# Moving five gate chunks of the first branch beside the attention in quarters three and four of a three-branch trunk layer

## The chip, the cores and the metric

The kernel runs on one core of a Trainium2 chip. The metric is device time in microseconds of one execution. The kernel before took 2836.89 us (median of three runs, 2834.71 to 2837.46). A difference of about 0.2% (5.7 us) is what a measurement of this kernel can tell from no change.

## The reference, cut to what matters

One layer runs over 2048 tokens of width 1024 with 16 meta tokens put in front. The normed tokens are projected once; three causal mixers of four heads (head size 128) work on the pieces, and each mixer's result goes through its own output matrix, is multiplied by a sigmoid gate, and is summed:

```
xn   = rms_norm(h);  proj = xn @ w_in
o_sb = stick_breaking_attention(q, k, v) * silu(sb_z)       # mixer 0: all earlier keys
o_gd = rms_norm(gated_delta_rule(q, k, v, beta, g)) * silu(gd_z)   # mixer 1: state over chunks
o_hg = rms_norm(hgrn2(q, k, v, log f)) * silu(hg_z)         # mixer 2: state over chunks
gate = sigmoid(mix)                                         # three of width 1024
y    = gate0 * (o_sb @ P0) + gate1 * (o_gd @ P1) + gate2 * (o_hg @ P2)
out  = h + y @ w_out
```

In the attention the work of a query block grows with the number of keys before it, so the later a quarter of the sequence, the longer its attention. The queries and keys of the delta rule go through a short causal convolution, which is VectorE work.

## The kernel before, in words

The tokens go through in four quarters of 512 (`nq` is 4, `TQ` is 512). Within a quarter two streams of work are woven together.

The first stream is dense work, the generator `dense_work`. It is cut into chunks: `proj` (a chunk is 24 matmuls of 512 columns; three matmuls per block of 128 make up for the precision of one, `mm3`, lines 166 to 169). In order: the attention's four projections for each head (`sb_proj`), a small projection for the delta rule's rates (`gdn_rows`, evacuated at L628), the delta rule's query, key and value chunks with their convolutions (`gdn_proj` with `conv`: twelve chunks, evacuated by ScalarE at L725, then three VectorE multiply-adds each at L730 and a product at L734), the first branch (`branch` with b = 0), the delta rule's gates (`gdn_gates`), the projections of the third mixer (`hg_proj`, evacuated at L1046, L1058 and L1064) with pieces of branch one between them, branch two, and the output matrix (`outp`).

A `branch` has, for each of eight output blocks, a gate chunk (24 matmuls; the sigmoid on ScalarE at L1203 puts it into a tile) and a product (12 matmuls of the mixer's result with the output matrix, at L1217 multiplied by the gate). With `lag` of 0 gate and product of a block follow each other; with a `lag` of 4, as branch two has, four gates run ahead of the first product. In the first branch the gates lie in tiles of the tag "g", of which there are two, and the product writes y, which has the tag "y" with eight tiles. The products of the first branch need the attention of all four heads (`obs`).

The second stream is the scans: the attention (`sb_scan`: scores `z` on TensorE, sigmoids on ScalarE at L522 and L523, a scan on VectorE at L528, a product at L534 on VectorE or GpSimd, transposes `tr` at L558, the split into high and low part on ScalarE at L562 and VectorE at L118, and the products `av`), then the delta rule (`gdn_mats`; `gdn_scan` with the inversion of small matrices on VectorE, written to and read from memory at L899 and L902, transposed at L904, then block products at L920, L941, L944, L959 and L969, and the recurrence over four steps of 128 tokens at L991, L996, L1002 to L1005), and the third mixer (`hg_scan`).

Every dense piece ends by yielding `END`. The main loop at the end of the kernel says how many dense pieces are emitted beside each scan: `adv(n)` emits n pieces alone, `weave(scan, scan_us, n)` spreads n pieces over a scan in proportion to the table `US` of their costs. The order in which the code emits is a priority only: a scheduler then lists each engine's instructions by it and by its own model of when operands and tiles are free, and on the chip each engine runs its list in order. So a piece for which no tile is free stands later in the list than where it was emitted.

The tiles that matter: "D" (16 tiles of a quarter's row of 512 tokens, used by nearly every projection, among them the raw results of L628 and L725 and the evacuations of L1046, L1058 and L1064), "S" (21, used by the scans), "w2" (5 tiles of weights, 512 KB each, loaded by SyncE's queue at L140), three matmul result tiles "acc" and one "av" in PSUM.

## Time and profile before

| | |
|---|---|
| median of three runs | 2836.89 us |
| the profiled execution, its own time | 2834.65 us |
| its span, first to last instruction | 2832.9 us |
| TensorE busy (PE) | 2777.6 us, 98% |
| VectorE busy (DVE) | 1501.6 us, 53% |
| ScalarE busy (ACT) | 934.1 us, 33% |
| GpSimd busy (POOL) | 737.7 us, 26% |
| mean granted TensorE clock | 0.996 |
| quarters, by the last output addition at L1255 | end at about 702, 1372, 2082 and 2830 us |
| attention, by the sigmoids at L522 | 1402 to 1652 us in quarter three, 2112 to 2405 us in quarter four |
| convolutions, by L730 | 1531 to 1644 us in quarter three, 2262 to 2384 us in quarter four |

Times in the profile are from the span's start. PE is TensorE, PEld its weight loads, DVE VectorE, ACT ScalarE, POOL GpSimd, SP SyncE's queue of transfers. In a row of windows stand the stretch, its length and each engine's busy time in it with the count of instructions, then the granted clock, the share of the DMA engines and GB/s. A row of waits names who waited for whom, the total, the number of times and the longest. A row of the timeline has start, duration, the instruction, how many were merged, and in brackets the idle time before it with what ended it. Matmuls overlap: a record runs past the start of the next one.

### The profile page before, as it was taken

What the parts mean: (1) busy time and instruction counts of PE and PEld (TensorE: products, weight loads), DVE (VectorE), ACT (ScalarE), POOL (GpSimd) and SP (SyncE); (2) the same over time, 40 slices, a digit from 0 to 9 for tenths busy, and PEclk for the clock granted to TensorE, in tenths of its full rate; (3) what the DMA queues carried; (4) which work ended last, traced back from release to release, by engine and by line L of the source; (5) the groups of instructions that cost most, each with busy time, mean ns of one, the idle gap of its engine ahead of it and who ended that gap; (6) DMA issues with size and microseconds to landing.
All of it is one profiled execution on the core that took longest, in us unless ns stands there. A gap on an engine that the chain in (4) does not pass through costs nothing. (4 is left out here: it accounts for less than half of the span.)

```text
span 2832.9 us, 42113 instructions
## 1 busy us (share of the span) xinstructions
PE 2777.6 (98%) x15696; PEld 2318.5 (82%) x15696; DVE 1501.6 (53%) x2879; ACT 934.1 (33%) x2131; POOL 737.7 (26%) x1009
## 2 busy tenths in 40 slices
PE   7999999999999999999999999999999999999999
PEld 7898788888887888888887778888888777788887
DVE  5466638745367535543256754464325677627521
ACT  5554333243345212112244531211224555112110
POOL 4555214433132302112023330111212323302111
PEclk9999999999999999999999999999999999999999
DMA  7667746679554654447654356344764434653456
GB/s 261 230 210 242 257 153 212 228 249 323 186 172 151 193 163 134 149 141 248 228 179 159 132 167 183 119 146 144 245 209 149 135 116 139 206 151 124 152 155 209
DMA packets 199632, 520.64 MB, mean 184 GB/s; under 512 B 42432, under 2 KB 43520, under 8 KB 199428
## 3 DMA queue, kind: packets, MB, share of 16 engines
q1 hardware_dynamic: 199140, 517.88, 56.1%
q8 instruction: 124, 2.03, 0.3%
q14 instruction: 80, 0.66, 0.1%
q10 hardware_dynamic: 288, 0.07, 0.0%
HBM read 397.55 MB, written 120.31 MB: 183 GB/s over the span
## 5 line engine op out<-in xcount | busy, mean ns | idle before, releaser
L167 PE MATMUL acc<-xh,w 128*128 128x512 f32 (+2 forms) x2224 | 853.5, 384 | 5.9 <-DMA w<-wk 1.7
L168 PE MATMUL acc<-xl,w 128*128 128x512 f32 (+2 forms) x2224 | 837.8, 377 | 0.3 <-DVE xl L260 0.2
L169 PE MATMUL acc<-xh,w 128*128 128x512 f32 (+2 forms) x2224 | 836.2, 376 | 0.7 <-DVE w L118 0.7
L167 PEld LDWEIGHTS acc<-xh,w 128*128 128x128 f32 x2224 | 421.9, 190 | 80.5 <-DMA w<-wk 2.5
L169 PEld LDWEIGHTS acc<-xh,w 128*128 128x128 f32 x2224 | 421.5, 190 | 74.3 <-DVE w L118 1.4
L168 PEld LDWEIGHTS acc<-xl,w 128*128 128x128 f32 x2224 | 421.8, 190 | 68.4 <-DVE xl L260 1.3
L528 DVE TENSOR_TENSOR_SCAN S<-S,zero 128x128 f32<-128x128 f32 (+4 forms) x216 | 196.8, 915 | 129.3 <-ACT S L522 116.8
L118 POOL TENSOR_TENSOR w<-wraw,w 128x512 fp32r<-128x512 f32 x106 | 150.1, 1417 | 292.8 <-ACT w L147 262.1
L534 POOL TENSOR_TENSOR S<-S,S 128x256 f32<-128x256 f32 (+2 forms) x108 | 93.3, 864 | 355.9 <-DVE S L528 262.2
L147 ACT CAST w<-wraw 128x512 fp32r<-128x512 f32 x182 | 112.4, 618 | 140.0 <-PE acc L169 67.6
L522 ACT ACTIVATE S<-z,rq 128x128 f32<-128x128 f32 (+4 forms) x216 | 116.8, 541 | 125.8 <-PE z L169 80.4
L730 DVE SCALAR_TENSOR_TENSOR D<-D,cw,D 128x512 f32<-128x512 f32 (+1 forms) x144 | 123.8, 860 | 18.0 <-ACT D L728 15.9
L167 PE MATMUL av<-xh,w 128*128 128x512 f32 (+2 forms) x328 | 128.8, 393 | 1.1 <-ACT D L1050 1.1
L167 PE MATMUL acc<-ob,w 128*128 128x512 f32 x316 | 126.8, 403 | 2.1 <-ACT ob L401 1.4
L168 PE MATMUL av<-xl,w 128*128 128x512 f32 (+2 forms) x328 | 127.7, 389 | 0.0
L118 DVE TENSOR_TENSOR S<-tr,S 128x512 fp32r<-128x512 f32 (+4 forms) x176 | 104.9, 606 | 41.6 <-ACT S L562 41.2
L169 PE MATMUL av<-xh,w 128*128 128x512 f32 (+2 forms) x328 | 126.9, 387 | 0.0
L168 PE MATMUL acc<-ob,w 128*128 128x512 f32 x316 | 125.4, 398 | 0.0
L169 PE MATMUL acc<-ob,w 128*128 128x512 f32 x316 | 124.9, 396 | 0.0
L1221 POOL TENSOR_TENSOR y<-y,g 128x512 f32<-128x512 f32 x32 | 45.8, 1436 | 272.7 <-DVE g L1219 272.7
L523 ACT ACTIVATE S<-z,rq 128x128 f32<-128x128 f32 (+4 forms) x216 | 116.2, 538 | 1.0 <-POOL S L527 0.9
L562 ACT CAST S<-tr 128x512 fp32r<-128x512 f32 (+4 forms) x176 | 91.0, 529 | 63.0 <-PE tr L558 62.8
(384 smaller groups left out, 5039.4 us busy)
## 6 DMA issues: line engine op xcount, KB each, us to landing
w<-wk SPq DMA_DIRECT2D x555, 512.0 KB, 3.5
wk<-w SPq DMA_DIRECT2D x184, 512.0 KB, 3.5
wraw<-in_w_in_dram SPq DMA_DIRECT2D x142, 256.0 KB, 3.8
D<-in_xq_dram SPq DMA_DIRECT2D x56, 256.0 KB, 4.5
S<-rows SPq DMA_DIRECT2D x48, 256.0 KB, 4.9
S<-dv SPq DMA_DIRECT2D x48, 256.0 KB, 4.2
out_dram<-D SPq DMA_DIRECT2D x32, 256.0 KB, 4.7
S<-dk SPq DMA_DIRECT2D x24, 264.0 KB, 3.9
```

The lines of the kernel that those rows point to most:

```text
L118: (eng or nc.gpsimd).tensor_sub(out_, a, hi.bitcast(F32))
L147: nc.scalar.copy(hi, raw)
L167: nc.tensor.matmul(dst, lh, rh, start=first, stop=False)
L168: nc.tensor.matmul(dst, lh, rl, start=False, stop=False)
L169: nc.tensor.matmul(dst, ll, rh, start=False, stop=last)
L522: nc.scalar.activation(pc[:, :n], z[:, :n], AF.Sigmoid, scale=rq[:, NT + i : NT + i + 1])
L523: nc.scalar.activation(at[:, :n], z[:, :n], AF.Sigmoid, scale=rq[:, i : i + 1])
L528: nc.vector.tensor_tensor_scan(pc[:, 0:n][:, ::-1], pc[:, 0:n][:, ::-1], zero1.broadcast_to([P, n]), 1.0 if carry[i] is None else pc[:, n ...
L534: eng.tensor_mul(at[:, :n], at[:, :n], pc[:, 1 : n + 1])
L562: nc.scalar.copy(ath[:kw, cs_], tr[:kw, cs_])
L730: nc.vector.scalar_tensor_tensor(dst[:, c0:], raw[:, c0 + i : c0 + i + n], cw[:, ci, i : i + 1], dst[:, c0:], ALU.mult, ALU.add)
L1221: nc.gpsimd.tensor_add(y[e], y[e], g)
```

## The change

In quarters three and four (`AHEAD` is 2, so for j of 2 and 3) the first branch gets a lag of 5. Its first five gate chunks are emitted right behind the attention's projections, ahead of `gdn_rows` and `gdn_proj`; then, behind the delta rule's projections, three more pieces (gates five to seven with products zero to two), and behind the first `hg_proj` the five products that are left. The gates of these two quarters lie in "y" tiles, and the product is written over the gate. In quarters one and two everything stays. The main loop gets other counts in those quarters and the table of costs a second version, one after the other for two quarters each.

```
+        tag = "D" if b == 2 else ("y" if lag else "g")
+
         def gate(e):
-            gs[e] = slot("D", (P, TQ)) if b == 2 else slot("g", (P, TQ))
+            gs[e] = slot(tag, (P, TQ))
...
             if b == 0:
-                y[e] = slot("y", (P, TQ))
+                y[e] = g if lag else slot("y", (P, TQ))
                 nc.vector.tensor_mul(y[e], g, ps)
...
+    AHEAD = 2
...
+            ahead = 5 * (j >= AHEAD)
+            b0 = branch(j, xs, 0, obs, y, yh, yl, ahead)
+            yield from take(b0, ahead)
             yield from gdn_rows(j, xs, gst)
             yield from gdn_proj(j, xs, range(H), gst)
             pool_share[0] = 2
-            b0 = branch(j, xs, 0, obs, y, yh, yl)
-            yield from take(b0, 5)
+            yield from take(b0, 3 if ahead else 5)
             yield from gdn_gates(j, xs, range(H), gst)
-            yield from take(b0, 3)
+            if not ahead:
+                yield from take(b0, 3)
             yield from hg_proj(j, xs, 0, hst)
+            if ahead:
+                yield from take(b0, 5)
             b1 = branch(j, xs, 1, obs, y, yh, yl)
...
+    ) * AHEAD + (
+        [CHUNK_US] * 34 + [B_US] * 3 + [CHUNK_US] * 8 + [3 * END] * 5 + [CHUNK_US] * 4 + [B_US] * 2 + REST
+    ) * (nq - AHEAD)
...
-        us = sum((US + US)[ends[0] % len(US) :][:n])
+        us = sum(US[ends[0] :][:n])
...
+        adv(5 * (j >= AHEAD))
         for h in range(H):
             weave(gdn_mats(j, h, gst), 8.0, 3)
...
-        adv(5)
+        adv(4 if j >= AHEAD else 5)
...
-        adv(5)
+        adv(6 if j >= AHEAD else 5)
```

What this does to the lists of TensorE in quarter four is seen at two places. The first is in the attention of the second head. `acc` is the result of a dense chunk, `z`, `tr` and `av` are the attention's scores, transposes and value products; `xh` and `xl` are the normed tokens, `w` the weights. Before:

```order
L169 MATMUL z_21252<-S_21174,D_20356 128x512
L168 MATMUL acc_22232<-xl_20106,w_4570_22230 128x512
L169 MATMUL acc_22232<-xh_20105,w_4570_22230 128x512
L168 MATMUL av_20969<-S_21205,S_21043 128x512
L169 MATMUL av_20969<-S_21204,S_21044 128x512
L558 MATMUL tr_21272<-ident,S_21054 128x128
L558 MATMUL tr_21272<-ident,S_21080 128x128
```

Now, at the same scores (`z` is of the same step):

```order
L169 MATMUL acc_22230<-xh_19983,w_4560_22228 128x512
L167 MATMUL z_21244<-S_21166,D_20347 128x512
L168 MATMUL z_21244<-S_21167,D_20347 128x512
L167 MATMUL av_20961<-S_21196,S_21035 128x512
L169 MATMUL z_21244<-S_21166,D_20348 128x512
L167 MATMUL acc_22230<-xh_20021,w_4560_22228 128x512
L168 MATMUL acc_22230<-xl_20022,w_4560_22228 128x512
L169 MATMUL acc_22230<-xh_20021,w_4560_22228 128x512
L167 MATMUL acc_22230<-xh_20059,w_4560_22228 128x512
L168 MATMUL av_20961<-S_21197,S_21035 128x512
```

Before, `acc_22232` is the first convolution's chunk, and behind its last matmul 99 rows of attention follow without a dense one, up to the second convolution's chunk. Now `acc_22230` is a gate chunk, the second of five, and the longest run of attention rows without a dense one in this quarter has 35. The last value product of the fourth head stands at row 11020 before, with three gate chunks of the first branch ahead of it, and at row 11156 now, with eight.

The second place is in the delta rule's scan of quarter four, at its block products. Before, with `acc_24555` and `av_24632` two chunks of the third mixer's first head:

```order
L169 MATMUL acc_24555<-xh_20105,w_5019_24553 128x512
L167 MATMUL av_24632<-xh_19839,w_5035_24628 128x512
L969 MATMUL z_24158<-S_22977,S_23965 64x64 x4
L969 MATMUL tr_24169<-S_23393,S_23966 64x64 x4
L991 MATMUL z_24200<-Sg_404,S_22947 128x128
L991 MATMUL tr_24202<-Sg_405,S_23145 128x128
L168 MATMUL av_24632<-xl_19840,w_5035_24628 128x512
L169 MATMUL av_24632<-xh_19839,w_5035_24628 128x512
```

Now, with `acc_24768` the last chunk for which a result tile is left:

```order
L168 MATMUL acc_24768<-xl_20098,w_5043_24766 128x512
L169 MATMUL acc_24768<-xh_20097,w_5043_24766 128x512
L959 MATMUL z_24190<-S_24042,S_23124 64x64 x4
L959 MATMUL z_24190<-S_24042,S_23322 64x64 x4
L959 MATMUL tr_24200<-S_24043,S_23540 64x64 x4
L959 MATMUL tr_24200<-S_24043,S_23739 64x64 x4
L969 MATMUL z_24216<-S_23124,S_24042 64x64 x4
L969 MATMUL tr_24227<-S_23540,S_24043 64x64 x4
L991 MATMUL z_24251<-Sg_404,S_23094 128x128
L991 MATMUL tr_24253<-Sg_405,S_23292 128x128
```

Behind these, the scan's 76 rows from L959 up to the last step's L996 stand without a dense matmul between them; before, the longest such run in this scan has 31 rows, the third step and the first half of the fourth. In quarter three the longest such run has 42 rows now and 31 before.

## The prediction

> **What bounds the kernel now.** I read the page first, then the windows by stage, then what TensorE waited for in the stages where it stood idle, then the timeline there. The page:

> ```profile
> span 2832.9 us, 42113 instructions
> PE 2777.6 (98%) x15696; PEld 2318.5 (82%) x15696; DVE 1501.6 (53%) x2879; ACT 934.1 (33%) x2131; POOL 737.7 (26%) x1009
> ```

> TensorE is busy for all but 55 us, so the change, which adds and removes no matmul, can win only where TensorE waits. The windows of quarters three and four (stretch, length, then busy time of PE, PEld, DVE, ACT, POOL, the granted clock, DMA share and GB/s) say where that is:

> ```profile
> core 0: us, PE busy (x) PEld busy (x) DVE busy (x) ACT busy (x) POOL busy (x), PEclk, DMA share, GB/s
> ...
> 1402.00:1519.00 117.00, 117.00 (x621) 96.64 (x621) 64.20 (x97) 54.48 (x115) 28.40 (x55) 1.00 0.52 176
> 1519.00:1663.00 144.00, 136.79 (x690) 109.34 (x688) 101.03 (x161) 77.75 (x166) 43.59 (x83) 0.99 0.40 133
> 1663.00:2112.00 449.00, 447.53 (x2505) 371.99 (x2506) 202.92 (x445) 84.11 (x216) 79.72 (x100) 1.00 0.57 178
> 2112.00:2216.00 104.00, 103.95 (x538) 84.92 (x537) 60.90 (x87) 50.36 (x100) 29.40 (x49) 1.00 0.50 163
> 2216.00:2249.00 33.00, 30.28 (x162) 23.68 (x161) 20.71 (x33) 17.80 (x38) 8.33 (x18) 1.00 0.28 97
> 2249.00:2317.00 68.00, 64.69 (x326) 52.27 (x325) 49.99 (x75) 39.48 (x80) 19.50 (x36) 1.00 0.45 148
> 2317.00:2334.00 17.00, 14.26 (x75) 10.84 (x75) 14.48 (x22) 10.00 (x22) 3.55 (x13) 0.90 0.09 32
> 2334.00:2384.00 50.00, 47.66 (x235) 38.36 (x234) 40.32 (x56) 29.80 (x60) 17.19 (x23) 1.00 0.46 155
> 2384.00:2414.00 30.00, 28.50 (x153) 22.66 (x151) 15.27 (x27) 13.40 (x31) 4.38 (x13) 1.00 0.39 118
> 2414.00:2833.00 419.00, 413.84 (x2342) 343.87 (x2342) 184.78 (x416) 68.47 (x189) 74.49 (x90) 1.00 0.53 166
> ```

> The first 117 us of quarter three's attention and the first 104 of quarter four's have no idle TensorE: attention projections stand beside them. Idle time comes later, 7.2 us in quarter three (144.00 - 136.79) and 2.7, 3.3, 2.7, 2.3 and 1.5 = 12.5 us in quarter four. Behind the attentions it is 1.5 us in 449 and 5.2 in 419. So the change is played for some 20 us.

> Two of these windows have a cause that the change touches. In 2216 to 2249 the DMA engines carry 97 GB/s and in 2317 to 2334 only 32: no weights are read, since no dense chunk stands in the list there. The timeline shows why in the first of them:

> ```profile
> 2218.92 0.39 PE L623 MATMUL acc<-xl,w 128*128 128x512 f32 x1
> 2245.97 0.29 PE L169 MATMUL z<-S,D 128*128 128x272 f32 x1
> 2247.05 0.59 ACT L628 COPY D<-acc 100x512 f32<-100x512 f32 x1
> ```

> The rates' chunk ends its matmuls at about 2219, and its evacuation into a "D" tile runs 28 us later, right behind the second head's last scores, which read that head's queries out of a "D" tile. All 16 are held, so the dense stream stands still, and TensorE has only the attention, each step of which it then waits for:

> ```profile
> PE av L168 <- DVE S L118: 1.5, 4, 0.7
> PE z L167 <- ACT S L523: 0.7, 1, 0.7
> PE av L167 <- ACT S L562: 0.4, 2, 0.2
> ```

> **The change part by part.** *The gates in the hole.* Gate chunks evacuate into "y" tiles, which nobody holds then, and need no "D". A gate costs TensorE 24 matmuls, and the timeline gives their spacing:

> ```profile
> 2333.72 0.39 PE L167 MATMUL acc<-xh,w 128*128 128x512 f32 x1
> 2333.95 0.39 PE L168 MATMUL acc<-xl,w 128*128 128x512 f32 x1
> ```

> 0.23 us apart, so a chunk is 5.5 us and five are 28 us, which take nothing off and add nothing: they are only done elsewhere. In the list the 99 rows without a dense matmul are gone. What that saves is the waiting in that window: 2.7 us of idle time, plus what the idle time hides. A record is 0.39 us though the next could start after 0.23, so each of the seven waits loses 0.16 us more: 1.1 us. Sum 3.8 us; bounds 2 and 4.

> *The second hole*, 2317 to 2334, has 55 such rows before and at most 35 now. It has 2.7 us idle and four waits (0.6 us), and a slow clock:

> ```profile
> PE tr L558 <- POOL S L534: 1.7, 1, 1.7
> 2331.80 0.63 PE L168 MATMUL acc<-xl,w 128*128 128x512 f32 x1
> 2332.23 0.63 PE L169 MATMUL acc<-xh,w 128*128 128x512 f32 x1
> ```

> Matmuls start 0.43 us apart, for about five of them: 1.0 us more. Sum 4.3 us; as a run of 35 rows stays, I take three quarters, 3.2 us, with bounds 0 and 5. [...]

> *The convolutions.* They are put later, not away. Their VectorE price stays:

> ```profile
> L730 DVE SCALAR_TENSOR_TENSOR D<-D,cw,D 128x512 f32<-128x512 f32 x36 | 29.9, 832 | 2.5 <-ACT D L728 1.9
> PE av L168 <- DVE S L118: 2.9, 2, 1.6
> ```

> The second row is of 1519 to 1663: the low part of the weights waits on VectorE behind multiply-adds of 832 ns, and TensorE behind it. In the list of VectorE, between the first and the last multiply-add of the convolutions, stand 29 attention scans (L528) in quarter four before and now: nothing gained there, and the 7.1 us (3.3, 2.3 and 1.5) stay. In quarter three there are 26 before and 21 now, since the last convolution falls behind the attention: 5/26 of 7.2 us is 1.4 us gained; bounds -3 (later heads hit worse) and 5.

> *The products without gates.* In both quarters the products three to seven now follow each other, four in a row: 12 matmuls, 2.8 us, for 512 KB of weights, 187 GB/s. The row of the end of quarter three has more than that with TensorE full:

> ```profile
> 2000.00:2082.00 82.00, 82.00 (x361) 66.62 (x360) 32.26 (x46) 17.22 (x28) 14.80 (x13) 1.00 0.79 259
> ```

> So nothing; if weights came late, up to 1 us a quarter. The gate's sigmoid on ScalarE is one per gate either way, and ScalarE is at 46 to 59% in the attention (54.48 of 117.00, 10.00 of 17.00). Five gates' weights more, 5 MB, pass SyncE's queue in windows of 97 and 32 GB/s, ahead of nothing urgent.

> *The delta rule's scan.* Here the moved gates are missing as cover. Up to L920 the count is about kept: from the fourth head's last product to L920 stand 316 rows before and 311 now. The margin there before is:

> ```profile
> 2481.69 0.47 SPq L899 DMA_DIRECT2D ud<-inv  x1
> 2490.80 0.71 DVE L904 STREAM_TRANSPOSE S<-S 128x512 f32<-128x512 f32 x1 [5.55 <-DMA S<-ud]
> 2494.83 1.20 PE L920 MATMUL z<-S,S 32*32 32x32 f32 x64
> ```

> 3.3 us from the transpose's end, of which five rows of 0.23 take 1.2. L899 now stands on SyncE's queue behind the weights of the third mixer's second head, whose tile comes free with the last product, 48 rows or 11.1 us ahead of L920; from L899 to the transpose's end it took 9.8 us. It just holds: nothing, or 3 us if it does not. Behind L959 in quarter four, TensorE has only the scan for 76 rows, 45 more than before. Of a recurrence step without cover the trace has an example:

> ```profile
> 2548.76 0.39 PE L991 MATMUL z<-Sg,S 128*128 128x128 f32 x2
> 2553.53 0.39 PE L991 MATMUL z<-Sg,S 128*128 128x128 f32 x2
> ```

> 4.77 us, in which TensorE runs 20 products as 40 records 0.11 us apart, 4.46 us: four heads cover each other, and a step loses 0.3. The two steps more without cover cost 0.6 us. For the block products the hand-overs are:

> ```profile
> 2503.12 0.63 ACT L948 COPY S<-z 32x256 f32<-32x256 f32 x2 [2.28 <-PE z L944]
> 2505.89 0.29 DVE L951 COPY S<-z 32x128 f32<-32x128 f32 x1 [0.32 <-ACT S L950]
> 2509.23 0.58 ACT L962 COPY S<-z 64x512 f32<-64x512 f32 x1 [1.64 <-PE z L959]
> 2510.17 0.70 DVE L962 COPY S<-tr 64x512 f32<-64x512 f32 x1 [1.85 <-PE tr L959]
> ```

> The copies behind L944 take 3.1 us, the list has 12 dense matmuls, 2.8 us, for them, and the halves overlap; the copy of 0.70 behind L959 leaves about 0.4 to wait, the next one 0.3. Together 1.0 us. The term is 1.6 us; bounds 0.5, and 16 if nothing overlapped (below).

> **Sum:** 3.8 + 3.2 + 1.4 - 1.6 = 6.8 us faster. The profiled execution took 2834.65 us (span 2832.9 and 1.75 around it), 2.2 us under the median of the three runs, within their spread; I take the 6.8 us off the median: **2830 us**.

> **The rivals.**

> *The holes only move (no measurable change).* The five gates use up the dense work that needs no "D" tile, and the convolutions behind them meet the same shortage at a later head; the list's run of 35 rows and four of 20 to 26 speak for it, the shorter longest run against. Then hole one pays half, the second nothing, quarter three nothing: 1.9 - 1.6 = 0.3 us, 2836 us, with -4 to +4.

> *The attention becomes covered altogether (faster).* The eight gates that now stand ahead of the attention's end spread over quarter four, and nearly all waits of the two windows' lists close: 7.2 + 12.5 us idle, of which three quarters is 15, less 1.6: 2823 us. For it: in the first parts of both attentions the projections leave no idle time at all. Against it: there VectorE is at 55 to 59% (64.20 of 117.00, 60.90 of 104.00), while beside the convolutions it is at 70 to 85%, and convolutions stay beside attention.

> *The scan pays more than the holes (slower).* In quarter four the delta rule's scan runs alone for 76 rows. Each step hands over at four kinds of rows:

> ```profile
> 2516.08 0.42 DVE L972 COPY S<-tr 64x256 f32<-64x256 f32 x1 [5.21 <-PE tr L969]
> 2516.72 0.29 DVE L994 TENSOR_TENSOR r<-D,tr 128x128 f32<-128x128 f32 x1
> 2530.67 0.27 ACT L1000 COPY r<-tr 128x128 f32<-128x128 f32 x1
> 2532.08 0.35 DVE L1008 SCALAR_TENSOR_TENSOR Sg<-Sg,gl,tr 128x128 f32<-128x128 f32 x1
> ```

> If hand-overs did not overlap between heads, the copies at L948 to L951 (3.1), L962 (0.58 and 0.70), L972 (four of 0.4) and a step's first eight (four of 0.29, four of 0.27: 2.2) would come after each other: 8.2 us less 2.8 of cover, and three steps at 3.6 us (2.2 and four of 0.35): 16 us. With 8.4 us gained that is 2844 us. It decides from a price of 8.4 + 5.7 = 14 us on, or 6 where the holes pay nothing. The row of 4.77 us speaks against it.

> **How the numbers follow.** The forecast (2826 to 2833) gets 0.46, the covered attention 0.15, no change 0.27, the scan 0.12. Three quarters of the forecast's own range lie beyond 5.7 us (0.2%, what a measurement of this kernel can tell from no change): 0.34 and 0.15 make 0.49 faster; 0.12 and 0.27 make 0.39 the same; 0.12 slower. The range goes from 2820, in the covered case, to 2840: it leaves out the scan's case and half of the covered one, 0.2.

> **What would show it.** Right: five sigmoids of L1203's kind in quarter four around 2220 to 2250 with DMA over 150 GB/s and TensorE full there; no stretch under 50 GB/s in the attention and no half clock; waits of `av` on L118 during the convolutions as before; a scan of quarter four with waits of 0.2 to 0.5 us, 1 to 3 us together. Wrong: idle time in quarter four's attention still over 10 us; L920 or the block products waiting for more than 5 us; quarters one and two other than by 1 us, as their lists do not change.

## The result, and the profile after

The changed kernel takes **2816.69 us** (median of five runs, 2813.5 to 2820.17) against 2837.46 for the kernel before in the same session (five runs, 2834.71 to 2838.58): a ratio of 0.9928, 95% interval 0.9915 to 0.9942, 20.8 us faster. The forecast was 2830 us with a range of 2820 to 2840: the right direction, too little of it.

The profiled execution of the changed kernel took 2820.17 us, the slowest of its five, and that of the kernel before 2834.65, nearly its fastest. So the two traces differ by 14.5 us; the other 6.3 lie between these executions and their medians. The page after:

```profile
span 2818.4 us, 42087 instructions
PE 2774.7 (98%) x15696; PEld 2319.9 (82%) x15696; DVE 1497.7 (53%) x2879; ACT 934.1 (33%) x2131; POOL 740.7 (26%) x1009
```

By the last output additions, the quarters' lengths and TensorE's idle time in their attentions are, for all profiled executions that the text uses (the idle times change by up to 1 us with where an attention is taken to end):

| kernel (median, us) | Q1 | Q2 | Q3 | Q4 | idle in attention, Q3 | Q4 |
|---|---|---|---|---|---|---|
| before (2837.46) | 702.3 | 669.6 | 709.9 | 748.1 | 7.0 | 12.9 |
| after (2816.69) | 703.6 | 669.5 | 700.0 | 742.2 | 0.7 | 6.9 |
| q3_only (2825.87) | 702.1 | 669.5 | 700.0 | 751.7 | 0.7 | 13.0 |
| q4_only (2826.5) | 698.8 | 669.7 | 710.7 | 739.5 | 6.9 | 7.0 |
| before_18_D (2846.51) | 719.7 | 669.5 | 701.6 | 750.8 | 0.1 | 12.0 |
| before_wraw2 (2856.38) | 722.1 | 669.8 | 711.9 | 749.3 | 7.5 | 12.6 |
| gates_in_D (2868.45) | 702.5 | 669.5 | 720.3 | 771.8 | 3.2 | 14.8 |
| before_v_apart (2822.14) | 702.7 | 669.5 | 697.6 | 748.0 | 0.2 | 8.4 |
| before_one_tap (2820.35) | 701.3 | 669.5 | 700.8 | 742.2 | 1.1 | 9.5 |
| before_v_conv (2820.08) | 702.9 | 669.6 | 697.1 | 749.0 | 0.2 | 10.2 |
| gates_behind (2830.89) | 701.8 | 669.7 | 708.2 | 748.3 | 6.1 | 11.1 |
| gates_behind_v_apart (2815.5) | 703.1 | 669.8 | 698.7 | 738.3 | 0.2 | 4.5 |
| after_v_apart (2809.74) | 701.0 | 669.7 | 699.9 | 733.6 | 0.7 | 2.7 |
| q4_only_v_apart (2810.74) | 702.3 | 669.5 | 697.9 | 736.3 | 0.2 | 2.8 |
| from_quarter_two (2828.51) | 702.2 | 677.1 | 699.9 | 739.4 | 0.8 | 7.0 |

In the traces quarter three gives 9.9 us and quarter four 5.9. The windows after, to be read against those of before:

```profile
core 0: us, PE busy (x) PEld busy (x) DVE busy (x) ACT busy (x) POOL busy (x), PEclk, DMA share, GB/s
1404.00:1519.00 115.00, 115.00 (x607) 94.86 (x607) 63.88 (x96) 52.86 (x111) 28.52 (x59) 1.00 0.53 179
1519.00:1658.00 139.00, 138.28 (x703) 111.53 (x702) 91.25 (x144) 75.90 (x158) 38.39 (x76) 1.00 0.46 150
2104.00:2208.00 104.00, 103.97 (x535) 84.86 (x535) 60.60 (x87) 49.62 (x99) 29.70 (x50) 1.00 0.50 164
2208.00:2256.00 48.00, 48.00 (x245) 40.00 (x245) 21.04 (x29) 20.05 (x40) 7.42 (x18) 1.00 0.41 139
2256.00:2400.00 144.00, 138.24 (x695) 111.27 (x694) 105.78 (x162) 82.85 (x167) 45.36 (x74) 0.99 0.44 143
2400.00:2428.00 28.00, 26.21 (x141) 21.02 (x140) 14.07 (x22) 11.26 (x26) 5.04 (x11) 1.00 0.41 122
2490.00:2550.00 60.00, 57.63 (x517) 49.18 (x516) 28.91 (x99) 16.47 (x64) 5.97 (x12) 0.97 0.37 105
```

Three things are seen. The convolutions' part of quarter three (second row) idles 0.7 us where it idled 7.2. The first hole of quarter four (2208 to 2256) is full: 48.00 of 48.00. From 2256 to the attention's end quarter four still idles 5.8 and 1.8 us. What TensorE waits for in the two attentions after, first quarter three, then four (waiter, releaser, total, times, longest):

```profile
PE acc L176 <- POOL nr L125: 0.4, 1, 0.4
PE acc L694 <- DVE D L683: 0.3, 1, 0.3
```

```profile
PE av L168 <- DVE S L118: 2.6, 4, 1.5
PE tr L558 <- POOL S L534: 1.9, 2, 1.4
PE acc L167 <- ACT ob L401: 1.4, 1, 1.4
PE av L167 <- ACT S L562: 1.1, 2, 0.7
...
```

The same two waits in quarter four's attention before:

```profile
PE av L168 <- DVE S L118: 5.3, 9, 1.6
...
PE av L167 <- ACT S L562: 1.3, 4, 0.4
```

In quarter three the attention's own waits (`av` on L118 and L562) are gone without rest; in quarter four 3.7 of 6.6 us stay. That is the difference to explain, for the convolutions stand beside the attention in both.

### The profile page after: what moved, and what is told of

Its sections match the earlier page's. It is cut to its first block, busy times and chain, and to the rows that moved or that the text cites. A ratio compares the mean times of both kernels' runs of the same rounds, so it can differ in the third digit from the quotient of the medians.

```text
span 2818.4 us, 42087 instructions
## 1 busy us (share of the span) xinstructions
PE 2774.7 (98%) x15696; PEld 2319.9 (82%) x15696; DVE 1497.7 (53%) x2879; ACT 934.1 (33%) x2131; POOL 740.7 (26%) x1009
## 5 line engine op out<-in xcount | busy, mean ns | idle before, releaser
L167 PE MATMUL acc<-xh,w 128*128 128x512 f32 (+2 forms) x2248 | 862.0, 384 | 4.0 <-DMA w<-wk 1.8
L168 PE MATMUL acc<-xl,w 128*128 128x512 f32 (+2 forms) x2248 | 850.0, 378 | 0.3 <-DVE xl L260 0.2
L169 PE MATMUL acc<-xh,w 128*128 128x512 f32 (+2 forms) x2248 | 847.6, 377 | 0.9 <-DVE w L118 0.9
L167 PEld LDWEIGHTS acc<-xh,w 128*128 128x128 f32 x2248 | 427.5, 190 | 78.7 <-DVE D L454 2.1
L169 PEld LDWEIGHTS acc<-xh,w 128*128 128x128 f32 x2248 | 427.3, 190 | 74.0 <-DVE w L118 1.6
L168 PEld LDWEIGHTS acc<-xl,w 128*128 128x128 f32 x2248 | 427.0, 190 | 70.1 <-issue 1.4
L528 DVE TENSOR_TENSOR_SCAN S<-S,zero 128x128 f32<-128x128 f32 (+4 forms) x216 | 196.6, 913 | 145.1 <-ACT S L522 125.2
L118 POOL TENSOR_TENSOR w<-wraw,w 128x512 fp32r<-128x512 f32 x106 | 149.6, 1413 | 295.2 <-ACT w L147 254.6
L534 POOL TENSOR_TENSOR S<-S,S 128x256 f32<-128x256 f32 (+2 forms) x108 | 94.5, 875 | 395.8 <-DVE S L528 269.1
L118 DVE TENSOR_TENSOR S<-tr,S 128x512 fp32r<-128x512 f32 (+4 forms) x176 | 104.8, 605 | 45.6 <-ACT S L562 45.1
L167 PE MATMUL acc<-ob,w 128*128 128x512 f32 x312 | 125.3, 403 | 1.8 <-ACT ob L401 1.4
L730 DVE SCALAR_TENSOR_TENSOR D<-D,cw,D 128x512 f32<-128x512 f32 (+1 forms) x144 | 119.7, 833 | 11.9 <-ACT D L728 9.6
L168 PE MATMUL acc<-ob,w 128*128 128x512 f32 x312 | 123.6, 397 | 0.0
L169 PE MATMUL acc<-ob,w 128*128 128x512 f32 x312 | 123.2, 395 | 0.0
L167 PE MATMUL av<-xh,w 128*128 128x512 f32 (+2 forms) x304 | 119.1, 392 | 1.1 <-ACT D L1050 1.1
L168 PE MATMUL av<-xl,w 128*128 128x512 f32 (+2 forms) x304 | 117.7, 387 | 0.0
L169 PE MATMUL av<-xh,w 128*128 128x512 f32 (+2 forms) x304 | 117.5, 387 | 0.0
L523 ACT ACTIVATE S<-z,rq 128x128 f32<-128x128 f32 (+4 forms) x216 | 115.9, 537 | 0.0
L562 ACT CAST S<-tr 128x512 fp32r<-128x512 f32 (+4 forms) x176 | 90.8, 529 | 59.8 <-PE tr L558 59.6
```

Of the source, the lines that this page charges most:

```text
L118: (eng or nc.gpsimd).tensor_sub(out_, a, hi.bitcast(F32))
L167: nc.tensor.matmul(dst, lh, rh, start=first, stop=False)
L168: nc.tensor.matmul(dst, lh, rl, start=False, stop=False)
L169: nc.tensor.matmul(dst, ll, rh, start=False, stop=last)
L523: nc.scalar.activation(at[:, :n], z[:, :n], AF.Sigmoid, scale=rq[:, i : i + 1])
L528: nc.vector.tensor_tensor_scan(pc[:, 0:n][:, ::-1], pc[:, 0:n][:, ::-1], zero1.broadcast_to([P, n]), 1.0 if carry[i] is None else pc[:, n ...
```

## The experiments

Three theories stood against each other. *Tiles*: dense chunks are held up because each needs one of the 16 "D" tiles; the moved gates lie in "y" tiles and need none. *Place*: the convolutions' VectorE work is moved past the heads that it hit. *Chance*: any new list shuffles the waits. Later a fourth came up, *supply*: how many dense chunks can stand beside an attention at all.

**Do the two quarters add up?** The change in quarter three alone (its table and counts for j of 3 those of before), and in quarter four alone:

```
-            ahead = 5 * (j >= AHEAD)
+            ahead = 5 * (j == AHEAD)
```

> The gates stand ahead in quarter three alone; quarter four is as before. Tiles theory (what cost time was that results of dense chunks and the halo copies waited for one of the 16 D tiles, in both quarters; the gates need none): the gain of quarter three in the profile of the change is kept, 10 us of its 709, so about 2827 us, and quarter four is as long as before, 748 us. Place theory (the convolutions' VectorE work is only moved past the heads it hit): about the same here. Chance theory (any new order of the lists shuffles the waits): quarter four, whose lists keep their order, is unchanged, and quarter three gains 10 as well, but the total is not the sum of the two quarters run alone. The prediction's term for this quarter, 1.4 us, would give 2836 us.

```
-    AHEAD = 2
+    AHEAD = 3
```

> The gates stand ahead in quarter four alone; quarter three is as before. Tiles theory: quarter four gains what it gained with both, 5 us in the profiled execution and up to 9 where the clock is not halved in its scan, so 2828 to 2832 us, and the sum of the two quarters alone is the gain of both, about 20 us. Chance theory: anything from 2825 to 2840 us, and no sum. The prediction's terms for this quarter, 3.8 and 3.2 less 1.6, would give 2832 us.

q3_only took 2825.87 us (ratio 0.9961, 0.9949 to 0.9974), q4_only 2826.5 (0.9966, 0.9952 to 0.9979): 11.4 and 10.7 us, 22.1 together, where the whole change gives 20.8. The quarter left alone keeps its idle time (13.0 and 6.9 us). Quarter four of q3_only is 751.7 us long in its trace where 748 had been expected: 10.2 us of it ran at half clock (0.98 of the clock granted from 2103 to 2407), before 3.4 (0.99 from 2112 to 2414); half of the difference, 3.4 us, is my estimate of what that costs. Parts that add up, each in its own quarter, speak against chance.

**More D tiles, no gate moved.** Two more D tiles in the room of two tiles for raw weights, and the control, which gives up that room alone:

```
-        "D": 16, "S": 21, "g": 2, "y": 8, "ob": 8,
+        "D": 18, "S": 21, "g": 2, "y": 8, "ob": 8,
...
-                    raw = wpool.tile([P, 512], F32, tag="wraw", name=nm("wraw"), bufs=4)
+                    raw = wpool.tile([P, 512], F32, tag="wraw", name=nm("wraw"), bufs=2)
```

> The kernel before, its order of emission untouched, with 18 D tiles for 16; the room comes from two of the four tiles for raw weights, which only quarter one uses, so quarters three and four are compared and quarter one may get slower. Tiles theory: the waits in the attention go without moving any gate; TensorE's idle time in the two attentions falls from 20 us to under 10, and quarters three and four together lose 8 us or more of 1458. Place theory and chance theory: the convolutions stand beside the same heads, so the idle time stays within 4 us of 20 and the quarters within 4 us of 1458.

> The kernel before with two instead of four tiles for raw weights and no more D tiles: the control for the run with 18 D tiles. All theories: quarter one is some 17 us longer, as there, quarters two to four stay within 2 us: about 2854 us.

They took 2846.51 us (1.0034, 1.0022 to 1.0047) and 2856.38 (two executions; 1.0068, 1.0049 to 1.0086). The room costs quarter one 19.8 us in the control's trace, where some 17 had been expected, and the two tiles alone are worth 9.9 us. In quarter three the idle time goes from 7 to 0.1 us with the order of emission of before: place is refuted there. In quarter four it hardly moves (12.0), so the expected 8 us in both quarters came out at 5.6: a miss for the tiles theory in quarter four.

**The same move without its tiles.** The gates moved, but in D tiles:

```
-        tag = "D" if b == 2 else ("y" if lag else "g")
+        tag = "D" if b == 2 or lag else "g"
...
-                y[e] = g if lag else slot("y", (P, TQ))
+                y[e] = slot("y", (P, TQ))
```

> The change with one thing undone: the five gates ahead lie in D tiles, as those of branch two, and the product writes a y tile of its own. Same work, same order of emission. Tiles theory: the gates now take from the 16 tiles and hold them to the attention's end, so the dense stream stalls earlier than before the change; the gain is lost and more, 2835 to 2850 us. Place theory: the gates still stand ahead of the convolutions, at least half of the gain stays, 2827 us or less.

2868.45 us (1.0112, 1.0098 to 1.0125), beyond what any theory expected. The gain is gone, as tiles said, but quarter four's idle time in the attention is only 1.9 us above before, and quarter three's is below it; most of the loss stands behind the attentions. More than half of the loss is clock (mean granted clock 0.986 over 2867.2 us, before 0.996 over 2832.9, by estimate some 29 us): the records show a stretch of 17.07 us at half clock behind each of the two attentions (0.98 granted from 1660 to 2092, 0.97 from 2420 to 2867), by estimate half of it, some 8.5 us, lost in each. TensorE now waits there in the delta rule's block products (quarter four, behind the attention):

```profile
PE z L941 <- DVE S L926: 2.2, 1, 2.2
...
PE z L920 <- DVE S L904: 1.4, 1, 1.4
```

These are waits of the scan that the forecast's slower rival spoke of, at rows ahead of those that it named. The run put five long-lived tiles more on D, so it does not show what the move costs with the number of tiles kept.

**D tiles for nothing.** The four raw weight tiles lie unused after quarter one. In quarters three and four each head's two value tiles go there, on the kernel before and on the changed one:

```
-        vh = slot("D", (P, TQ), F32R)
-        vl = slot("D", (P, TQ), F32R)
+        if j >= 2:
+            vh, vl = [wpool.tile([P, 512], F32R, tag="wraw", name=nm("v"), bufs=4) for _ in range(2)]
+        else:
+            vh = slot("D", (P, TQ), F32R)
+            vl = slot("D", (P, TQ), F32R)
```

> The order of the kernel before, unchanged. In quarters three and four alone, the two value tiles of each attention head (high and low part, held until the head's scan is over) stand in the four 2 KB tiles that receive raw weights in the first quarter and lie unused after it; the 16 D tiles so carry 9 instead of 11 tiles of each head. Tiles theory: TensorE's idle time in the attention falls from 7 to under 1 us in quarter three and from 13 to 7 or less in quarter four, quarters one and two stay as they are: 2820 to 2827 us, most of the change's gain without moving a gate. Place theory: the convolutions stand beside the same heads as before, so the idle times and the 2837 us stay within 3. Chance theory: any time within 10 us of 2837, with idle times that go either way.

> The changed kernel, with the same value tiles in the unused raw weight tiles in quarters three and four. Tiles theory: in quarter three there is nothing left to gain (0.7 us idle in the attention); of the 6.9 us in quarter four's attention some 3 to 5 are still waits on D tiles and go, so 2811 to 2815 us, a gain much smaller than on the kernel before. Place theory and chance theory: no reason for a gain, 2814 to 2820 us.

before_v_apart took 2822.14 us (0.9948, 0.9936 to 0.996): 14.8 us, 70% of the change's gain, without moving a gate. after_v_apart took **2809.74** (0.9906, 0.9893 to 0.9919), 7 us less than the changed kernel, the fastest of all and a little below what was expected. The two attentions of before, and of before_v_apart:

```profile
1402.00:1663.00 261.00, 253.79 (x1308) 205.98 (x1307) 165.23 (x257) 132.23 (x280) 71.99 (x138) 0.99 0.46 153
2112.00:2414.00 302.00, 289.35 (x1479) 232.73 (x1477) 201.67 (x297) 160.85 (x326) 82.36 (x150) 0.99 0.43 139
```

```profile
1402.00:1651.00 249.00, 248.83 (x1304) 204.06 (x1303) 164.46 (x258) 132.65 (x280) 72.23 (x138) 1.00 0.48 160
2100.00:2400.00 300.00, 291.55 (x1480) 234.42 (x1478) 199.85 (x298) 159.93 (x328) 84.41 (x150) 0.98 0.44 142
```

Quarter three does the same work on VectorE (165.23 and 164.46 us, 257 and 258 instructions) in 12 us less, so VectorE has the higher share and TensorE no wait. VectorE's load by itself does not make the waits. Of quarter four's idle time a third goes with the tiles and 8.4 us stay, where 7 or less had been expected. The length of quarter four does not fall in this trace (748.0 against 748.1): 17.1 us of it ran at half clock (0.94 granted from 2300 to 2400), before 3.4.

**VectorE's load, with tiles short.** The kernel before, with two of three multiply-adds of each convolution left out in quarters three and four:

```
-        for i in range(1, 4):
+        for i in range(1, 2 if j >= 2 else 4):
```

> The kernel before, order and tiles unchanged, but in quarters three and four each convolution does one of its three multiply-adds on VectorE (two of 832 ns left out, 24 a quarter, 20 us of VectorE's time beside the attention; the convolution's values are not those of the reference). The forecast's reading (VectorE's price beside the convolutions makes the waits): idle time in quarter three's attention falls from 7 to 3 us or less, quarter four's by 3 or more, 2826 to 2831 us. Tiles theory: the D tiles are held as long as before but for 1.7 us each, so the idle times stay within 1.5 us: 2833 to 2838 us.

2820.35 us (0.9941, 0.9927 to 0.9955): 16.5 us, more than either side expected. The tiles theory as it stood (no effect) is wrong: with the D tiles short, VectorE's multiply-adds do make the waits. Either relief is enough in quarter three: idle time falls to 1.1 us by less VectorE work and to 0.2 by more tiles. The timeline of before around the last of these waits shows how the two join (VectorE; start, duration, instruction):

```profile
1614.03 1.58 DVE L730 SCALAR_TENSOR_TENSOR D<-D,cw,D 128x512 f32<-128x512 f32 x1
1615.53 0.16 DVE L759 TENSOR_SCALAR aq<-nr 128x4 f32<-128x4 f32 x1
1615.64 1.54 DVE L730 SCALAR_TENSOR_TENSOR D<-D,cw,D 128x512 f32<-128x512 f32 x2
1617.10 0.42 DVE L118 TENSOR_TENSOR S<-tr,S 128x256 fp32r<-128x256 f32 x1
```

All three multiply-adds of one convolution stand ahead of the low part. A convolution starts when its raw tile comes free, and GpSimd's copy of the halo (L724) is its first step. How long that copy's engine stood idle ahead of it in quarter three, of before and of before_v_apart (where the line is L727):

```profile
L724 POOL COPY D<-halo x12: 185/206/1103, 1519.4 to 1630.0; 128x3 f32<-128x3 f32 x12
...
  PE acc L380: 14.9, 4
```

```profile
L727 POOL COPY D<-halo x12: 180/186/1191, 1508.7 to 1621.3; 128x3 f32<-128x3 f32 x12
...
  PE acc L380: 0.9, 1
```

Four copies of before wait 14.9 us for `acc L380`, transposes out of a D tile; with the value tiles apart one waits 0.9. Over all releasers it is 35.9 us against 8.2, in before_one_tap still 35.1 (so there the tiles stay short, and the waits go nevertheless), in after none in quarter three and 38.9 in quarter four (before 33.0). The delay itself can be worked out from the rows: from the end of the high part's copy on ScalarE to the start of its low part on VectorE, in the convolutions' stretch of quarter three (1519 to 1660), a mean over 27 to 29 of them: 0.98 us before, 0.59 in before_v_apart, 0.43 in before_one_tap, 0.71 after. So the delay falls with the tiles at equal VectorE work.

The delay is only half of the account. A wait is what is left of it when TensorE has done what its list puts beside it. The two steps of quarter three at which before waits for L118 are the 29th and the 42nd of 52; the same steps in other traces (dense matmuls are those of `xh` and `xl` between the last transposes ahead of the high part's copy and the value product that waits):

| kernel | delay, us (29th, 42nd) | dense matmuls | TensorE's wait, us |
|---|---|---|---|
| before | 1.53, 3.21 | 0, 2 | 1.56, 1.30 |
| before_18_D | 0.38, 2.77 | 14, 13 | 0, 0 |
| before_v_apart | 0.38, 2.39 | 14, 13 | 0, 0 |
| before_one_tap | 0.03, 0.03 | 12, 2 | 0, 0 |
| after | 1.10, 0.38 | 19, 18 | 0, 0 |

The product of the 42nd step, of before and of before_v_apart:

```profile
1615.91 0.36 PE L167 MATMUL av<-S,D 128*128 128x256 f32 x1
1617.57 0.39 PE L168 MATMUL av<-S,D 128*128 128x256 f32 x1 [1.30 <-DVE S L118]
```

```profile
1611.60 0.36 PE L167 MATMUL av<-S,v 128*128 128x256 f32 x1
...
1612.15 0.37 PE L168 MATMUL av<-S,v 128*128 128x256 f32 x1
```

At this step the low part is still 2.4 us late with the value tiles apart (2.8 in before_18_D), and TensorE does not wait, because 13 dense matmuls, 3.0 us at 0.23 each, stand where before has two. With fewer multiply-adds the same two matmuls are enough, because the delay is gone. So here free tiles remove the wait by letting dense work stand beside it, and less VectorE work removes it by shortening the delay; at the 29th step both changed at once. In the changed kernel it is the dense work again: 19 and 18 matmuls.

**Still more tiles in the order of before.** Besides the value tiles, the convolutions' raw inputs in "y" tiles:

```
-        raw = slot("D", (P, 3 + WQ))
+        raw = slot("y", (P, 3 + TQ)) if j >= 2 else slot("D", (P, 3 + WQ))
```

> The order of the kernel before, with the value tiles in the unused raw weight tiles and, besides, the convolutions' raw inputs in the y tiles, in quarters three and four. Twelve short-lived tiles a quarter leave the ring of 16 D tiles. Tiles theory: of the 8.4 us that TensorE still idles in quarter four's attention with the value tiles apart, 3 to 5 go, so 2815 to 2819 us. If what is left there belongs to the order (rows without dense work, VectorE beside the convolutions), it stays: 2820 to 2824 us.

2820.08 us (0.9943, 0.993 to 0.9955): no fall in quarter four's idle time (10.2 against 8.4), so what is left there is no shortage of D tiles but belongs to the order. TensorE's list says what: with the order of before and free tiles the first hole of 99 rows is gone, but one of 98 rows stands at the third head, and at the end of the fourth head the first branch's first three products hold the three result tiles until that head is done. In the order of before, with free tiles too, 26 chunks' worth of dense matmuls stand beside quarter four's attention; in the changed order 31 do. That is the supply theory.

**Place or supply?** The lag and the y tiles kept, the five gates emitted behind the delta rule's projections instead of ahead, with D tiles short and with the value tiles apart:

```
-            b0 = branch(j, xs, 0, obs, y, yh, yl, ahead)
-            yield from take(b0, ahead)
             yield from gdn_rows(j, xs, gst)
             yield from gdn_proj(j, xs, range(H), gst)
             pool_share[0] = 2
+            b0 = branch(j, xs, 0, obs, y, yh, yl, ahead)
+            yield from take(b0, ahead)
```

> The changed kernel, but in quarters three and four the five gate chunks in y tiles are emitted behind the delta rule's projections instead of ahead of them; lag, tiles and counts stay. TensorE's list of quarter four has the runs of 99 and 55 rows without a dense matmul of the kernel before again (the changed kernel: 35 at most), and 27 chunks' worth of dense matmuls beside the attention (before 26, changed 31). Tiles theory: the gates help only where they fill the time in which no D tile is free, which they do no longer: 5 to 8 us idle in quarter three's attention, 10 to 13 in quarter four's, 2831 to 2838 us. If the lag or the y tiles themselves were the cause, 2815 to 2822 us.

> The same, with the value tiles in the unused raw weight tiles in quarters three and four. The list of quarter four has one run of 98 rows and none above 30 besides, 29 chunks' worth of dense matmuls beside the attention (order of before with these tiles: 98 and 60, 26 chunks; changed order with these tiles: none above 30, 31 chunks). Tiles and supply (D tiles in both quarters, and in quarter four the number of dense chunks that can go before the first branch's products need the fourth head): quarter three under 1 us idle, quarter four between the 8.4 and the 2.7 us of those two, 4 to 7: 2813 to 2820 us. Place alone: as the kernel before, 2833 or more.

gates_behind took 2830.89 us (0.9982, 0.9973 to 0.9991), 0.1 us below what tiles expected, gates_behind_v_apart 2815.5 (0.9929, 0.9917 to 0.9942). The attentions of quarter four, of gates_behind, gates_behind_v_apart and after_v_apart in turn:

```profile
2110.00:2427.00 317.00, 305.90 (x1539) 246.58 (x1539) 202.31 (x298) 163.39 (x331) 82.71 (x150) 0.98 0.44 142
```

```profile
2102.00:2416.00 314.00, 309.49 (x1572) 250.57 (x1572) 200.22 (x297) 163.26 (x331) 84.34 (x150) 0.99 0.45 146
```

```profile
2101.00:2417.00 316.00, 313.22 (x1608) 255.10 (x1607) 202.61 (x298) 164.31 (x333) 87.87 (x150) 1.00 0.48 151
```

The number of matmuls in such a stretch is the supply: 1479 before, 1480 in before_v_apart, and here 1539, 1572 and 1608. With tiles short, the place ahead is worth 14.2 us (2830.89 to 2816.69), 8.2 of it in quarter three by the traces: there the gates fill the time in which no D tile is free. With tiles free, the lag, with its y tiles and its later products, gives 6.6 us (2822.14 to 2815.5) and the place 5.8 more (to 2809.74), and quarter three has nothing left to win.

**Where not to do it.** The changed order in quarter four alone, with the value tiles apart in both quarters; and the changed order from quarter two on:

```
-    AHEAD = 2
+    AHEAD = 3
```

> The changed order in quarter four alone, with the value tiles in the unused raw weight tiles in quarters three and four. Quarter three with its old order and these tiles took 697.6 us, with the new order and these tiles 699.9; quarter four with the new order and these tiles 733.6. Tiles theory, in which the quarters add up: 2806 to 2809 us, 1 to 4 under the changed kernel with these tiles. Chance theory: no better than 2810.

```
-    AHEAD = 2
+    AHEAD = 1
```

> The changed order from quarter two on. In quarter two's attention TensorE waits 0.4 us. Tiles theory: there is no wait there to remove, and the scan of the delta rule loses the gates as cover in one more quarter, so quarter two is 0 to 3 us longer: 2817 to 2820 us. Place theory says the same of the attention. Chance theory: quarter two may go either way by 10 us.

q4_only_v_apart took 2810.74 us (0.9906, 0.9893 to 0.992), level with after_v_apart at 2809.74, where 1 to 4 us less had been expected: a miss for the tiles theory, and what chance had expected (no better than 2810). In the traces quarter three is 2.0 us shorter, as expected, and quarter four 2.7 longer, at a mean granted clock of 0.997 over the whole span where after_v_apart has 0.998. from_quarter_two took 2828.51 (0.997, 0.996 to 0.998), 11.8 us worse than the change and 8.5 beyond the expectation. Quarter two is 7.6 us longer in its trace. Its attention gains nothing, and what TensorE waits for behind it, from 1010 to 1379, where before waits for nothing, is:

```profile
PE tr L380 <- DVE S L1032: 1.8, 3, 0.8
PE acc L167 <- ACT ob L401: 0.9, 1, 0.9
PE z L1126 <- DVE S L1117: 0.6, 1, 0.6
PE z L1135 <- DVE S L1117: 0.4, 1, 0.4
PE tr L991 <- DVE S L1012: 0.4, 1, 0.4
```

4.1 us of waits at the end of the delta rule's scan and in the third mixer's; I read them as the dense work spent early, which is missing there. The profiled execution (2823.34) was the fastest of eight, so 5 us of the median are not in this trace; what they are stays open.

## Why the prediction was wrong, step by step

- **What bounds the kernel** (TensorE's waits in the two attentions, "some 20 us"): right, and 20.8 us were won. That they are not all won is also true: 6.9 us of idle time stay in quarter four, while the waits removed gave back more than their idle time: quarter three lost 6.3 us of it and became 9.9 shorter.
- **The convolutions: "Their VectorE price stays"**: this is the step that failed, most of all in quarter three. The forecast gave it 1.4 us, as 5 of 26 scans fall outside; it gained 9.9 in the trace and 11.4 alone. The row of 2.9 us for `av` on L118 was read as VectorE's price as such. The runs show that it is VectorE's price *while D tiles are short* and TensorE's list has no dense work to put beside the delay (0 and 2 matmuls at the two waits): the same VectorE work costs 0.2 us of idle time once two tiles a head are elsewhere. The forecast had found the shortage in the first hole and did not ask whether it also stood behind the waits of the convolutions, whose raw results need the same tiles. In quarter four, where nothing was to be gained, some 3 us of idle time went too: outside the two holes 7.1 us before, about 4 after (1.7 and 2.4 in the first and last row shown under the second hole, without 1.4 us for `ob`, which stand behind the attention before). Tiles stay short there after the change (38.9 us idle ahead of L724).
- **The gates in the first hole**, 3.8 us: right. Five sigmoids (L1205) from 2215.90 to 2250.22, no idle time from 2208 to 2256. The DMA engines carry 139 GB/s there, not over 150.
- **The second hole**, 3.2 us: hardly paid. It is the end of the third head, now from 2333 to 2345:

```profile
2256.00:2333.00 77.00, 75.32 (x383) 60.71 (x382) 52.98 (x84) 43.60 (x90) 25.22 (x39) 1.00 0.47 152
2333.00:2345.00 12.00, 9.91 (x50) 7.59 (x49) 10.31 (x16) 6.33 (x13) 2.52 (x10) 0.86 0.13 44
2345.00:2428.00 83.00, 79.21 (x404) 63.99 (x403) 56.57 (x85) 44.18 (x92) 22.67 (x36) 1.00 0.45 143
```

```profile
2338.26 0.50 PE L558 MATMUL tr<-ident,S 128*16 128x128 f32 x3 [1.42 <-POOL S L534]
2339.21 0.49 PE L167 MATMUL av<-S,vmh 16*128 16x512 f32 x1 [0.45 <-ACT S L562]
2339.92 0.50 PE L168 MATMUL av<-S,vmh 16*128 16x512 f32 x1 [0.23 <-DVE S L118]
```

  Of 2.7 us of idle time 2.1 stay, three of the four waits among them, and so does the stretch of 3.4 us at half clock behind them. The DMA engines carry 44 GB/s there and the granted clock is 0.86, both of which the forecast's signs of being right had excluded. A shorter run of rows without dense matmuls did not take these waits away. Quarter four was forecast at 5.4 us for both holes, less the scan; the trace has 5.9 and the run of quarter four alone 10.7 by its median. That the trace comes so near is luck: some 2.6 us too much for the second hole and some 3 too little for the convolutions nearly cancel.
- **The products without gates**, nothing: no wait on weights stands in either attention's list. As forecast.
- **The delta rule's scan**, 1.6 us: mis-sized. "It just holds" did not: the forecast took L920's inputs as the margin, but it is the dense chunk behind L920 whose weights come late. The waits of the stretch behind the attention, and the timeline there:

```profile
PE acc L167 <- DMA w<-wk: 1.8, 1, 1.8
PE tr L969 <- DVE S L962: 0.5, 1, 0.5
```

```profile
2504.97 1.20 PE L920 MATMUL z<-S,S 32*32 32x32 f32 x64
2507.96 0.51 PE L167 MATMUL acc<-xh,w 128*128 128x512 f32 x1 [1.79 <-DMA w<-wk]
...
2509.96 0.63 PE L167 MATMUL acc<-xh,w 128*128 128x512 f32 x1
2510.39 0.63 PE L168 MATMUL acc<-xl,w 128*128 128x512 f32 x1
```

  2.3 us of waits and a stretch of half clock (matmuls 0.43 us apart for 3.4 us, a granted clock of 0.97 from 2490 to 2550; by estimate half of the 3.4 lost): 4.0 us. The steps of the recurrence without cover are 4.77 us apart, as worked out.
- **The rivals.** "The attention becomes covered altogether" (2823 us, 0.15) came nearest: it is what happened in quarter three. The argument against it was VectorE's share of 70 to 85% beside the convolutions. before_v_apart has the higher share (77% from 1519 to 1651, where before has 70%) and no waits, so that was no reason. "The scan pays more than the holes" is real where five more D tiles are held (gates_in_D) and where nothing is won in the attention (from_quarter_two), and small here.
- **The sum** against the profiled execution: 6.8 forecast, 14.5 measured. Quarter three's convolutions (8.5 more) and the scan (2.4 less) make 6.1 of the 7.7 between them; quarter four's convolutions and second hole nearly cancel, and the rest is within what two executions differ by. The last 6.3 us of the 20.8 lie in which executions were profiled. The range's lower end, 2820, rested on the covered case, 2823 us, with no allowance for half-clock stretches, of which the trace after has two of 3.4 us in quarter four, each behind waits.

Not settled: how much quarter four wins by itself. It is 10.7 us by the median of q4_only, 8.6 and 5.9 in two traces; executions of q4_only differ in the granted clock (2823.53 us at a mean of 0.997, 2829.4 at 0.995), and quarter one, which neither edit touches, alone goes from 698.8 to 703.6 us among these traces. Nor is it settled what from_quarter_two loses outside its trace.

## What to carry to other kernels

When an engine's work is seen ahead of a wait, ask also why the waiting engine has nothing else to do just then: a price read off "the engine is busy with X" is only that price while the shortage lasts that keeps other work away, and a run that frees the shortage at the same load tells the two apart (here 165.23 and 164.46 us of VectorE's work in quarter three's attention, with 7.0 and 0.2 us of TensorE's idle time). Before moving work to fill a hole, look for buffers that lie idle in that phase: here four tiles that are dead after the first quarter gave 14.8 us without moving anything, and 7 more on top of the change. What could be moved beside the long phase here was limited by what its products wait for (26 chunks, then 31), and cover spent where nothing waits was missed later (4.1 us of waits behind quarter two's attention in from_quarter_two).

## What the runs showed of the hardware that I had not expected

Before has one of the 17, at 1616.7 us: 2.58 us, most of three waits of 1.30, 1.19 and 0.91. After has one of the eight, at 2505.5: a single wait of 1.79 us, for weights. Single waits of 1.5 us, in the pieces at 1661.0 in before and at 2300.7 in after, were followed by full clock, while 1.21 us (before, at 2326.6) and 0.73 (after, at 2338.2) were followed by half clock, each with a piece of over 1.3 us ahead of it. So between 1.6 and 2.0 us of idle time in a piece came with 1.7 us more in eight cases (an estimate, half of 3.413) and with nothing in three; what decides between the two was not shown. The two stretches of 17.07 us, both in gates_in_D, cost some 8.5 us each by the same estimate; why they last so long stays open. Executions of one kernel differ in the clock: the changed kernel took 2820.17 us at a mean clock of 0.996 and 2813.5 at 0.999, 6.7 us less, and 0.003 of its time is some 8 us.
